# Low halves of the second layer's feed-forward weights by a sign-turned ScalarE cast and an accumulating transfer

## The chip, the cores and the metric

The kernel runs on one core of a Trainium2 chip. The metric is the device time of one execution in microseconds (us). The core has five engines that run on their own and meet through semaphores: TensorE (PE in the profile) for matrix products, with its weight loads shown apart as PEld; VectorE (DVE); ScalarE (ACT); GpSimd (POOL); and SyncE (SP), which here only issues transfers. Transfers between the chip's DRAM and the on-chip memory, and inside that memory, run on 16 DMA engines whichever engine issued them.

## The reference, cut to what matters

A decoder trunk of two layers on 512 tokens of width 1024, all in float32. Each layer is a token mixer, a layer norm, a feed-forward network and a second layer norm. The change touches the feed-forward network of the second layer alone:

```python
def sqrelu_mlp(x, w1, b1, w2, b2):
    return jnp.square(jax.nn.relu(x @ w1 + b1)) @ w2 + b2
...
ffn = sqrelu_mlp(x, ffn_w1[layer], ffn_b1[layer], ffn_w2[layer], ffn_b2[layer])
x = layer_norm(DEEPNORM_ALPHA * x + ffn, ln2_g[layer], ln2_b[layer])
```

`w1` is 1024 x 4096 and `w2` 4096 x 1024, so each layer has 32 MB of feed-forward weights.

## The kernel before, in words

**Split products.** TensorE multiplies in a rounded float32 format (fp32r). To keep float32 accuracy every operand is split in a high half, the value rounded to that format, and a low half, what the rounding lost. A product is the sum of three: high x high, high x low, low x high. So each weight, once loaded, goes through two instructions: ScalarE casts the raw tile to the high half (L101), VectorE subtracts the high half from the raw tile to get the low half (L102).

**Units, chunks and slots.** The class `Weights` hands out the weights in units of 128 x 1024 values (512 KB), in the order of use. `_prep` makes a unit ready: it fetches the raw chunk if it isn't there (L71, issued on SyncE), then the cast and the subtraction. A raw chunk lies in one of two buffers (`bufs=2` in `fetch`), so the load of a chunk waits until the chunk two before has been read by its last reader. The two halves lie in one of eight slots (three and five, `add_slots`), so a unit's cast waits until TensorE is done with the unit eight before. `next` asks for units up to `ahead`, here 5, in front of the one in use; the compiler that schedules the program may bring them forward on an engine's queue, up to the eight slots. Once compiled, each engine works its queue in that fixed order.

**The second layer's feed-forward.** It runs in five blocks of 8, 8, 6, 4 and 6 tiles of 128 hidden columns (`FFN_BLOCKS[1]`). In a block, the f tiles come first (`ffn1`, products at L225): a tile takes one unit of the first weight, 24 products, then ScalarE's Relu (L154), VectorE's square, ScalarE's cast (L215) and VectorE's low half (L216). The f tiles have two accumulation banks (`stp`), so the Relu of a tile must be over before the next tile but one begins. Then come the products with the second weight, named g (L1311), in the last block h (L1295), 8, 8, 6, 4 and 6 units of 24 products each, added by VectorE to the residual. The first six f tiles of block one use units that were split earlier and kept in DRAM; they are brought back by GpSimd transfers (L88). In the first block the residual is also turned by TensorE and copied back by ScalarE (L1287) before the g products.

The units of the first weight (key `"f11"`, 26 of them) have 128 columns of a chunk of 256, so two units share a 1 MB chunk and each partition's slice is eight pieces of 512 bytes. The units of the second weight (key `"f21"`, 32) are a chunk of 512 KB each, 4 KB in one piece on every partition.

**Order by hand.** Where a layer norm is near, `fence` keeps both instructions of a unit behind an instruction of the norm (`i0`, `i1`). It binds the scheduler only and adds no wait.

Of the kernel before, what the change touches and what calls it, by code (L numbers as in the profile page):

```python
# [9 lines left out]
F32 = mybir.dt.float32  # L10
# [3 lines left out]
ALU = mybir.AluOpType  # L14
# [29 lines left out]
KEEP_FROM = 8  # L44
AHEAD = (5, 4)
FJ = 3
BEFORE = (1, 3, 1, 2)
MIX_BUFS = (3, 4, 1, 3, 3)
WARM = 24
# [6 lines left out]
class Weights:  # L56
# [23 lines left out]
    def _prep(self, n):  # L80
        nc = self.nc
        while self.done < min(n, len(self.units)):
            key, src, nk, ncol, off, width = self.units[self.done]
            if key[0] == "split":
                pool, s = self.slots[self.done % len(self.slots)]
                w = tuple(pool.tile([P, nk, ncol], F32R, tag=f"w{x}{s}", name=f"w{x}{self.done}", bufs=1) for x in ("hi", "lo"))
                for x, d in zip(w, self.kept[key[1]]):
                    nc.gpsimd.dma_start(x, d)  # L88
                self.ready[self.done] = w
                self.done += 1  # L90
                continue
            self.fetch(self.done)
            raw = self.chunk[key][:, :, off : off + ncol]
            pool, s = self.slots[self.done % len(self.slots)]
            hi = pool.tile([P, nk, ncol], F32R, tag=f"whi{s}", name=f"whi{self.done}", bufs=1)
            lo = pool.tile([P, nk, ncol], F32R, tag=f"wlo{s}", name=f"wlo{self.done}", bufs=1)
            if key[0] == "q":
                i0 = nc.scalar.mul(hi, raw, 0.125).ins
                i1 = nc.vector.scalar_tensor_tensor(lo, raw, 0.125, hi.bitcast(F32), op0=ALU.mult, op1=ALU.subtract).ins
            else:  # L100
                i0 = nc.scalar.copy(hi, raw).ins  # L101
                i1 = nc.vector.tensor_sub(lo, raw, hi.bitcast(F32)).ins  # L102
            if self.fence:
                self.tc.add_manual_dep(i0, self.fence[0], NOSYNC, reason="behind the layer norm")
                self.tc.add_manual_dep(i1, self.fence[1], NOSYNC, reason="behind the layer norm")
            self.ready[self.done] = (hi, lo)
            self.done += 1
# [58 lines left out]
def kernel(ctx: ExitStack, tc: tile.TileContext, a: dict, out: bass.AP):  # L166
# [780 lines left out]
    def ln_to_x(ln, c0, c1, g, b, xs, others):  # L947

        r = ln.norm(X, c0, c1, others)
        for j in range(KT):  # L950
            y, (xh, xl) = X[j][:, c0:c1], (t_[:, c0:c1] for t_ in xs[j])
            stt(y, y, pv(g[0], g[1] + j), r, ALU.mult, ALU.mult)
            bj = pv(b[0], b[1] + j)
            la = act(xh, y, AF.Identity, bias=bj)
            lv = V.scalar_tensor_tensor(xl, y, bj, xh.bitcast(F32), op0=ALU.add, op1=ALU.subtract).ins
        W.fence = (la.name, lv.name)
# [62 lines left out]
    def tail_norm_lead(xk, name, bias, g, b, lead_n, lead_name, then=None):  # L1019
# [7 lines left out]
        lead = Lead(lead_n, xs, lead_name)  # L1027
        ln_to_x(ln, *HALVES[0], g, b, xs, [lambda n=n: t.run(n) for n in BEFORE[:2]])
        t.run(2 * KT - t.done)
        ln_to_x(ln, *HALVES[1], g, b, xs, [lambda n=n: lead.run(n) for n in BEFORE[2:]])  # L1030
        return xs, lead.finish()
# [170 lines left out]
    def normalised(h, j0, j1):  # L1202
# [12 lines left out]
        if j1 == KT:  # L1215
            out(KT - 1)
            if h == 0:
                W.fence = split_done[h, FJ]

# [161 lines left out]
```

## Time and profile before

| | |
|---|---|
| times shown | 1183.87 and 1185.64 us, median 1184.76 |
| span of the profiled execution | 1181.7 us, that is 2.2 to 3.9 under the times shown, which count what lies around the span; its own whole time is not listed apart from these |
| TensorE busy | 1154.5 us, 98% |
| VectorE, ScalarE, GpSimd busy | 752.0, 507.9, 66.5 us |
| second layer's feed-forward after its first six tiles | 851 to 1174 us of the span |
| transfers over the whole span | 169.60 MB |

The page gives the busy time of each engine, the span in slices, the transfer queues, the chain of work that ended last, and the costliest groups of instructions as "line engine operation out<-in". The trace behind it can be asked for one tile, for a stretch of time or for an engine's waits. A row with "<-" at its end tells what released the engine from its idle time. A duration of one instruction includes its pipeline, so two that follow one another can overlap by a tenth of a microsecond.

### The profile page before, as it was taken

What the parts mean: (1) busy time and instruction counts of PE and PEld (TensorE: products, weight loads), DVE (VectorE), ACT (ScalarE), POOL (GpSimd) and SP (SyncE); (2) the same over time, 40 slices, a digit from 0 to 9 for tenths busy, and PEclk for the clock granted to TensorE, in tenths of its full rate; (3) what the DMA queues carried; (4) which work ended last, traced back from release to release, by engine and by line L of the source; (5) the groups of instructions that cost most, each with busy time, mean ns of one, the idle gap of its engine ahead of it and who ended that gap; (6) DMA issues with size and microseconds to landing.
All of it is one profiled execution on the core that took longest, in us unless ns stands there. A gap on an engine that the chain in (4) does not pass through costs nothing.

```text
span 1181.7 us, 17927 instructions
## 1 busy us (share of the span) xinstructions
PE 1154.5 (98%) x7252; PEld 966.1 (82%) x7252; DVE 752.0 (64%) x1332; ACT 507.9 (43%) x802; POOL 66.5 (6%) x125
## 2 busy tenths in 40 slices
PE   9989999999999999999999999899999999999997
PEld 7777767799888888888999776699988888888885
DVE  7999875498546546546565999886933433434446
ACT  6857769345434435434323122662741422413220
POOL 1022210000000000000021110001000000000000
PEclk9999999999999999999999999999999999999999
DMA  8511221332689678788464641215242232323211
GB/s 211 166 55 50 81 81 46 109 114 72 223 292 299 228 281 298 249 292 290 134 213 153 205 164 58 68 44 172 90 143 72 89 125 72 109 91 104 78 47 72
DMA packets 132547, 169.60 MB, mean 144 GB/s; under 512 B 13874, under 2 KB 105778, under 8 KB 132464
## 3 DMA queue, kind: packets, MB, share of 16 engines
q1 hardware_dynamic: 123664, 136.96, 36.0%
q0 software_dynamic: 8640, 31.46, 7.9%
q8 instruction: 57, 0.93, 0.3%
q14 instruction: 26, 0.21, 0.1%
q10 hardware_dynamic: 160, 0.03, 0.0%
HBM read 132.12 MB, written 35.65 MB: 142 GB/s over the span
## 4 chain that ended last, share of the span: by engine, by line
PE 83%; ACT 2%; DVE 1%; DMA 1%; issue 1%; POOL 0%; SPq 0%; DVEq 0%; ACTq 0%
PE f L225 24%; PE g L1311 12%; PE acf L225 11%; PE fl L225 5%; PE tlb L225 4%; PE tld L225 4%; PE pv L225 3%; PE h L1295 3%; PE pg L225 3%; PE cw L1126 3%; PE tla L225 2%; PE pl L225 2%; PE acmo L225 1%; PE gg L225 1%; PE gv L225 1%
## 5 line engine op out<-in xcount | busy, mean ns | idle before, releaser
L102 DVE TENSOR_TENSOR wlo<-raw,whi 128x1024 fp32r<-128x1024 f32 x176 | 213.3, 1223 | 196.1 <-ACT whi L101 193.0
L101 ACT CAST whi<-raw 128x1024 fp32r<-128x1024 f32 x176 | 182.3, 1050 | 319.6 <-PE g L1311 107.0
L1311 PE MATMUL g<-whi,hh 128*128 128x512 f32 x208 | 81.7, 393 | 0.0
L1311 PE MATMUL g<-whi,hl 128*128 128x512 f32 x208 | 81.6, 392 | 0.0
L1311 PE MATMUL g<-wlo,hh 128*128 128x512 f32 x208 | 81.6, 392 | 0.0
L225 PE MATMUL f<-xah,whi 128*128 128x512 f32 x208 | 81.0, 390 | 0.0
L225 PE MATMUL f<-xdh,whi 128*128 128x512 f32 x208 | 81.0, 389 | 0.0
L225 PE MATMUL f<-xdl,whi 128*128 128x512 f32 x208 | 80.9, 389 | 0.0
L225 PE MATMUL f<-xal,whi 128*128 128x512 f32 x208 | 80.9, 389 | 0.0
L225 PE MATMUL f<-xdh,wlo 128*128 128x512 f32 x208 | 80.9, 389 | 0.0
L225 PE MATMUL f<-xah,wlo 128*128 128x512 f32 x208 | 80.9, 389 | 0.0
L225 PE MATMUL acf<-hh,whi 128*128 128x512 f32 x192 | 75.6, 394 | 0.0
L225 PE MATMUL acf<-hl,whi 128*128 128x512 f32 x192 | 75.5, 393 | 0.0
L225 PE MATMUL acf<-hh,wlo 128*128 128x512 f32 x192 | 75.4, 393 | 0.0
L215 ACT CAST hh<-fr 128x512 fp32r<-128x512 f32 x64 | 39.7, 621 | 59.1 <-DVE fr L353 59.1
L216 DVE TENSOR_TENSOR hl<-fr,hh 128x512 fp32r<-128x512 f32 x64 | 44.1, 690 | 31.1 <-ACT hh L215 31.1
L353 DVE TENSOR_TENSOR fr<-fr 128x512 f32<-128x512 f32 x64 | 43.6, 684 | 16.7 <-ACT fr L154 16.7
L357 DVE SCALAR_TENSOR_TENSOR cy<-hp,wdw,cy 128x512 f32<-128x512 f32 (+1 forms) x75 | 49.3, 657 | 0.8 <-ACT cy L154 0.8
L88 POOL DMA_DIRECT2D whi<-kepth x30 | 16.0, 535 | 549.5 <-PE tlb L225 385.9
L1311 PEld LDWEIGHTS g<-whi,hh 128*128 128x128 f32 x208 | 39.1, 188 | 8.8
L1311 PEld LDWEIGHTS g<-wlo,hh 128*128 128x128 f32 x208 | 39.1, 188 | 8.8
L1311 PEld LDWEIGHTS g<-whi,hl 128*128 128x128 f32 x208 | 39.0, 188 | 8.8
(631 smaller groups left out, 2891.9 us busy)
## 6 DMA issues: line engine op xcount, KB each, us to landing
raw<-in_ffn_w_dram SPq DMA_DIRECT2D x48, 1024.0 KB, 5.5
raw<-in_ffn_w_dram SPq DMA_DIRECT2D x32, 512.0 KB, 3.8
kepth<-whi SPq DMA_DIRECT2D x30, 512.0 KB, 3.2
keptl<-wlo SPq DMA_DIRECT2D x30, 512.0 KB, 9.2
whi<-kepth POOLq DMA_DIRECT2D x30, 512.0 KB, 3.6
wlo<-keptl POOLq DMA_DIRECT2D x30, 512.0 KB, 4.6
raw<-in_conv_w_pw_dram SPq DMA_DIRECT2D x12, 1024.0 KB, 6.5
raw<-in_mix_w_in_dram SPq DMA_DIRECT2D x16, 512.0 KB, 4.2
```

What stands on the lines that cost most here:

```text
L88: nc.gpsimd.dma_start(x, d)
L101: i0 = nc.scalar.copy(hi, raw).ins
L102: i1 = nc.vector.tensor_sub(lo, raw, hi.bitcast(F32)).ins
L215: i0 = S.copy(hi, src).ins
L216: i1 = V.tensor_sub(lo, src, hi.bitcast(F32)).ins
L225: ins = PE.matmul(ps[:, c0:c1], u[:, k, ksl], v[:, c0:c1], start=start and k == 0 and i == 0, stop=stop and k == n - 1 and i == 2).ins
L353: V.tensor_tensor(o, x, y, op=op)
L357: V.scalar_tensor_tensor(o, x, s, y, op0=op0, op1=op1)
L1126: PE.matmul(cps[j, c0][g][C, :], Ds[j][t // 16][R, t % 16, :], hps[j][R, t + c0 : t + c1], start=t < 4, stop=t >= n - 4, tile_position=(R. ...
L1295: PE.matmul(ps, u, v, start=k == 0 and i == 0, stop=k == nk - 1 and i == 2)
L1311: PE.matmul(pss[b], u, v[:, kk, :], start=k + kk == 0 and i == 0, stop=k + kk == nb - 1 and i == 2)
```

## The change

For the units of the two keys in `BY_DMA`, all of the second layer's feed-forward weights that are split there, the low half is made in another way. ScalarE writes minus the raw tile, rounded, into the low tile; then GpSimd issues a transfer from the raw tile onto the low tile that adds instead of overwriting. Minus the rounded value plus the value is what the subtraction gave. VectorE's subtraction falls away for these units. The instruction held by the fence (`i1`) is now the ScalarE one. The other weights are split as before.

```diff
+BY_DMA = ("f11", "f21")
...
                 i0 = nc.scalar.copy(hi, raw).ins
-                i1 = nc.vector.tensor_sub(lo, raw, hi.bitcast(F32)).ins
+                if key[0] in BY_DMA:
+                    i1 = nc.scalar.mul(lo, raw, -1.0).ins
+                    nc.gpsimd.dma_start(lo, raw, accum_op=ALU.add)
+                else:
+                    i1 = nc.vector.tensor_sub(lo, raw, hi.bitcast(F32)).ins
```

## The prediction

> **What bounds the kernel now.** I read the page's busy times, then busy time by stage, then the chain of waits that ended last.
>
> ```profile
> span 1181.7 us, 17927 instructions
> PE 1154.5 (98%) x7252; PEld 966.1 (82%) x7252; DVE 752.0 (64%) x1332; ACT 507.9 (43%) x802; POOL 66.5 (6%) x125
> ...
> 851.00:1140.00 289.00, 288.98 (x1282) 237.74 (x1281) 120.13 (x138) 91.42 (x115) 0.00 (x0) 1.00 0.31 98
> ...
> 865.90 44.28 PE g L1311 x192
> 910.18 43.52 PE f L225 x192
> ```
>
> TensorE is the chain. In the 289.00 us of the second layer's feed-forward it is busy for 288.98, while VectorE is busy for 120.13, ScalarE for 91.42 and GpSimd for nothing. The chain there is "f" and "g" products alone: a first-weight tile takes 43.52 / 8 = 5.44 us, a second-weight unit 44.28 / 8 = 5.54 us. VectorE's subtractions are off this chain, so their price can come back at most as the idle time of TensorE, 0.02 us here. The question is thus not what VectorE saves, but whether the new way delivers the low halves in time, and what it holds up.
>
> **What is removed and added.** The rows of the raw tiles in the second half of the trace, and the nearest rows for the new parts:
>
> ```profile
> L101 ACT CAST whi<-raw x58: 1035/1053/1061, 833.3 to 1129.2; 128x1024 fp32r<-128x1024 f32 x58
> L102 DVE TENSOR_TENSOR wlo<-raw,whi x58: 1214/1225/1228, 834.8 to 1130.3; 128x1024 fp32r<-128x1024 f32 x58
> ...
> L98 ACT ACTIVATE whi<-raw x4: 1045/1058/1063, 25.9 to 106.4; 128x1024 fp32r<-128x1024 f32 x4
> 809.45 0.54 POOL L88 DMA_DIRECT2D wlo<-keptl  x1
> ```
>
> The 58 units are the 26 of the first weight that are not kept and the 32 of the second. VectorE loses 58 x 1.225 = 71 us. ScalarE gains 58 scaled copies; the nearest row is the same shape times 0.125, 1.058 us, so 61 us, of which 58 x 0.96 (two such instructions start 0.96 apart, rows below) count: 91 + 56 = 147 of 289 us at most, still half idle. GpSimd gains 58 issues of 0.54 us or more. Nothing else stands in its queue: the last of its transfers (809.45) is over before the first new one. So what waits behind a waiting issue is only the next low half.
>
> The low half no longer needs the high one, only its own scaled copy. Per unit it is ready 0.96 + L after the high half where it was 1.23, with L the time from the issue of the accumulating transfer to its landing. TensorE takes a unit eight units later (eight slots), some 43 us, so L itself is hidden. What is not hidden is the **raw buffer**.
>
> ```profile
> SPq L71 <- DVE wlo L102: 743.9, 99, 257.8
> ...
> 942.68 1.05 ACT L101 CAST whi<-raw 128x1024 fp32r<-128x1024 f32 x1 [1.87 <-PE f L225]
> 943.64 0.68 ACT L154 ACTIVATE fr<-f,PV 128x512 f32<-128x512 f32 x1
> 945.62 0.62 ACT L215 CAST hh<-fr 128x512 fp32r<-128x512 f32 x1 [1.31 <-DVE fr L353]
> 948.12 1.05 ACT L101 CAST whi<-raw 128x1024 fp32r<-128x1024 f32 x1 [1.88 <-PE f L225]
> ...
> raw<-in_ffn_w_dram SPq DMA_DIRECT2D x8, 512.0 KB, 3.8
> ...
> raw<-in_ffn_w_dram SPq DMA_DIRECT2D x48, 1024.0 KB, 5.5
> ```
>
> SyncE's load of the next raw chunk waits for the last reader of the chunk two before, VectorE's subtraction today: that is the 743.9 us row. With the change the last reader is the accumulating transfer. And on ScalarE the cast of a unit stands ahead of the Relu of the tile just finished (942.68, then 943.64). A cast that waits for its load holds back the Relu, and TensorE has two banks for these tiles.
>
> While the f tiles run, the units cast are second-weight ones, a chunk of their own each. One buffer's round is then: cast and scaled copy 2 x 0.96 and a hand-over, 2.0; the transfer, L; the next load 3.8. It has to fit in two tiles, 10.88 us, so **L up to 5.1 us costs nothing**. Today the same round is 1.05 + 1.23 + 3.8 = 6.1.
>
> No accumulating transfer is in the trace. The rows around it, all 512 KB:
>
> ```profile
> q1 hardware_dynamic: 123664, 136.96, 36.0%
> q0 software_dynamic: 8640, 31.46, 7.9%
> ...
> kepth<-whi SPq DMA_DIRECT2D x30, 512.0 KB, 3.2
> keptl<-wlo SPq DMA_DIRECT2D x30, 512.0 KB, 9.2
> whi<-kepth POOLq DMA_DIRECT2D x30, 512.0 KB, 3.6
> wlo<-keptl POOLq DMA_DIRECT2D x30, 512.0 KB, 4.6
> ```
>
> Bounds for L are 3.2 us (out of SBUF, the first of a pair) and 9.2 us (out of SBUF, the second). I take 4.6: issued by GpSimd, onto the same tile, with another transfer in flight, which comes nearest. The round is then 2.0 + 4.6 + 3.8 = 10.4, inside 10.88: **0 us** in the steady stretches; at 9.2 it is 15.0, 4.1 too long.
>
> A page speaks against this. The Trainium skill, "Collectives: The Full Stack", section "The bandwidth ceiling: the fold count and why AG ≠ RS ≠ AR", says that an add in the DMA engine needs two source reads where a copy needs one, and that this halves the rate. By it the data part of the 3.6 us row (144 packets, 9 an engine, at 0.079 x 16 x 1181.7 / 8640 = 0.173 us, so 1.56 us) would count twice, L would be 5.2 and the round 11.0, late by 0.1 us: 12 rounds cost 1 us, inside ScalarE's slack. The sum stays as it is; no row here shows an add.
>
> **The start.** In the first block the prefetch is not yet ahead:
>
> ```profile
> 837.14 22.09 SPq L71 DMA_DIRECT2D raw<-in_ffn_w_dram  x7
> ...
> 833.30 1.98 ACT L101 CAST whi<-raw 128x1024 fp32r<-128x1024 f32 x2
> ...
> 840.81 1.05 ACT L101 CAST whi<-raw 128x1024 fp32r<-128x1024 f32 x1
> ...
> 862.59 1.05 ACT L101 CAST whi<-raw 128x1024 fp32r<-128x1024 f32 x1 [1.54 <-DMA raw<-in_ffn_w_dram]
> 863.54 0.68 ACT L154 ACTIVATE fr<-f,PV 128x512 f32<-128x512 f32 x1
> 864.12 1.55 ACT L1287 COPY X<-xt 128x512 f32<-128x512 f32 x3
> ...
> DMA raw<-in_ffn_w_dram: 4.5, 3
> ```
>
> The chunk of the first two units is free at 837.14 today. With the change its scaled copies end at 833.30 + 4 x 0.96 = 837.2, the second transfer is issued 0.54 behind the first and lands 4.6 later: 842.5. The load behind it lands at 846.3, and with rounds of 10.4 the units 3, 5 and 7 of the second weight are cast at 856.7, 867.1 and 877.5, where unit 7 is cast at 862.59 today. TensorE wants unit 7 at 865.90 + 7 x 5.54 = 904.7 and its low half is there by 884, so weights don't run out. But the Relu at 863.54 and the copies of the turned residual at 864.12, which the first g products need, stand on ScalarE behind these casts today. If that order stays, they wait until 879.5: **15 us**. If the late casts are ordered behind them: **0**. I take **4.5 us**, by the row of this very stretch that is nearest: three casts there wait 4.5 us in all for their loads, so the order lets a cast stand that much ahead of its data.
>
> **Sum.** Span 1181.7 + 0 (steady) + 4.5 (start) - 0.02 at best = 1186.2. The median shown, 1184.76, is 3.1 above the profiled span, so the forecast is **1189.3 us**.
>
> **The rivals.**
> Fully hidden: the order on ScalarE follows the loads and L is 5.1 or less. For it speaks that TensorE has 43 us of prefetch, against it the start. 1184.8 us.
>
> First-weight transfers are cut small. Their raw slice is 128 of 256 columns, eight pieces of 512 bytes a partition against one of 4 KB. If GpSimd's issue grows with the pieces it is 8 x 0.54 = 4.3 us; 64 pieces an engine at the 0.36 x 16 x 1181.7 / 123664 = 0.055 us of queue 1 are 3.5 us, 1.9 more than 1.56. L is then 4.6 + 3.8 + 1.9 = 10.3 for these. A chunk of two has 4 x 5.54 = 22.2 us and needs 5.5 (its load) + 5.54 (until the second unit's turn) + 2.0 + 10.3 = 23.3: 1.2 late, six rounds, 7 us. The start is 9.4 later, by the share taken above (4.5 of 15) 3 more, so 7. 1184.8 + 14 = 1199 us. Against it: 0.54 us for 128 pieces may be mostly fixed.
>
> Slower: the **round through the raw buffer becomes the bound** in the f tiles. At L = 9.2 it is 15.0 against 10.88. The f tiles of blocks 2 to 5 have 24 second-weight units cast in front of their Relus, 12 rounds x 4.1 = 49 us, less the slack: a Relu ends 2 x 0.96 + 0.68 = 2.6 after its tile and must be over by 5.44, so 2.8 in each of four blocks, 11. That leaves 38. The start has unit 7 cast at 850.9 + 3 x 15.0 = 895.9, a bound of 34, by the same share 10. 1184.8 + 48 = 1233 us. It begins at L = 5.1 and passes 2% (23.7 us, about what a measurement tells from no change) near 12 x (L - 5.1) - 11 + 6 = 23.7, so L = 7.5. For it: the 9.2 row, the transfer reads two tiles and writes one, and loads share the 16 engines (share 0.31 now). Against it: 9.2 is reached behind a sister transfer, and by a write to DRAM.
>
> Faster: only a rearranged order elsewhere could do it; TensorE idles 0.02 us in the stretch.
>
> The change does what it says by the code: minus the rounded weight plus the weight is the old low half.
>
> **How the numbers follow.** Forecast 1189.3: 0.40. Hidden, 1185: 0.14. Small pieces, 1199: 0.13. Buffer round, 1233: 0.32. Faster: 0.01. The first three lie within 2%: 0.67. The range runs from 1182.5 (hidden, and the spread of the two times) to 1238, just past the buffer's price; beyond it L above 9.2 is left out.
>
> **What would show it.** Right: 118 subtractions left at the old line; 58 scaled copies of 1.06 us; 58 issues on GpSimd and a landing near 4.6 us; SyncE's loads waiting for that transfer, not for VectorE; ScalarE's casts waiting for loads a few us more, all near 860; TensorE's idle time before the first g product only. Wrong: landings above 7 us, casts in every f stretch waiting for raw loads, and TensorE idle before f tiles with the Relu as releaser.

## The result and the profile after

The changed kernel takes **1244.29 us** (1244.08 to 1244.5), against 1184.76 before: a ratio of 1.0511, 95% interval 1.0471 to 1.0551. That is 59.5 us slower, past the upper end of the range. The page of the changed kernel, its busy times, the chain that ended last, and two of its transfer rows:

```profile
span 1242.8 us, 18061 instructions
PE 1166.1 (94%) x7252; PEld 971.4 (78%) x7252; DVE 684.9 (55%) x1274; ACT 559.2 (45%) x860; POOL 133.6 (11%) x183
...
PE 50%; DMA 25%; issue 7%; ACT 7%; DVE 7%; SPq 2%; POOL 1%; ACTq 0%; DVEq 0%; POOLq 0%
...
wlo<-raw POOLq DMA_DIRECT2D x58, 512.0 KB, 7.1
raw<-in_ffn_w_dram SPq DMA_DIRECT2D x32, 512.0 KB, 4.5
```

VectorE is relieved by 67 us (the sum had 71). But a quarter of the chain is now transfers, where before they were 1% of it and TensorE 83%. The adds land 7.1 us after their issue at the median, and the second-weight loads, 3.8 us in the same row before, take 4.5.

Busy time of the changed kernel in two stretches, the start of the second layer's feed-forward and what follows (columns as in the prediction: length, busy time of PE, PEld, DVE, ACT and POOL, granted clock, share of the DMA engines, GB/s):

```profile
851.00:910.00 59.00, 44.59 (x205) 37.05 (x204) 10.11 (x15) 32.55 (x43) 12.09 (x11) 0.88 0.75 162
910.00:1140.00 230.00, 197.07 (x824) 159.04 (x823) 37.30 (x54) 87.66 (x104) 41.60 (x35) 0.93 0.85 164
```

TensorE is idle for 14 us of the first and 33 us of the second. Before, it was idle for 0.02 us of both together. Who waits for whom in the changed kernel (total time in us, times, longest), and the casts of the 58 units, with what they waited for (total time in us, times):

```profile
PE f L230 <- ACT fr L159: 35.6, 9, 12.2
...
SPq L72 <- DMA wlo<-raw: 592.7, 43, 268.9
...
L102 ACT CAST whi<-raw x58: 1030/1047/1056, 830.7 to 1191.8; 128x1024 fp32r<-128x1024 f32 x58
...
  DMA raw<-in_ffn_w_dram: 186.2, 34
```

All 43 loads issued here wait for an adding transfer (the longest wait, 268.9 us, is that of the first load, which stood ready long before this stage). 34 of the 58 casts wait for a load, 186.2 us in all, where before it was 3 casts and 4.5 us. TensorE waits nine times for the Relu of an f tile. The casts stretch over 361 us; before it was 833.3 to 1129.2, 296 us, and there 48 of them waited for TensorE to free their slots. The two raw buffers are the bound now.

One round of a raw buffer, in the second block's f tiles. First the rows of ScalarE, then GpSimd's issue, then the load from the chain, then the landings of the adds from 946 to 995 us (smallest, median, largest):

```profile
970.66 1.05 ACT L102 CAST whi<-raw 128x1024 fp32r<-128x1024 f32 x1 [3.90 <-DMA raw<-in_ffn_w_dram]
971.61 0.68 ACT L159 ACTIVATE fr<-f,PV 128x512 f32<-128x512 f32 x1
972.19 1.05 ACT L104 ACTIVATE wlo<-raw 128x1024 fp32r<-128x1024 f32 x1
...
983.97 1.05 ACT L102 CAST whi<-raw 128x1024 fp32r<-128x1024 f32 x1 [3.25 <-DMA raw<-in_ffn_w_dram]
```

```profile
973.53 0.88 POOL L105 DMA_DIRECT2D wlo<-raw  x1 [6.15 <-ACT wlo L104]
```

```profile
980.00 3.88 DMA raw<-in_ffn_w_dram
```

```profile
DMA to landing us min/median/max: 4.5/6.3/7.6
```

The cast starts at 970.66. The scaled copy does not follow it: the Relu goes in between, and the add is issued at 973.53, 2.9 us after the cast. It lands 6.4 us later, the load starts at 980.00, and the next cast from this buffer is at 983.97. The round is 13.3 us, against 10.88 us for two tiles; the other rounds of this stretch are 11.9 to 14.1 us. And the Relu of each tile stands behind such a cast, as in the second row.

The first-weight units, two to a chunk, are worse. Casts at 1002.62 and again, from the same buffer, at 1027.61; GpSimd's issues in between, and their landings from 1004 to 1033 us:

```profile
1002.62 1.05 ACT L102 CAST whi<-raw 128x1024 fp32r<-128x1024 f32 x1 [8.48 <-DMA raw<-in_ffn_w_dram]
...
1027.61 1.06 ACT L102 CAST whi<-raw 128x1024 fp32r<-128x1024 f32 x1 [17.30 <-DMA raw<-in_ffn_w_dram]
```

```profile
1004.92 1.57 POOL L105 DMA_DIRECT2D wlo<-raw  x1 [10.00 <-ACT wlo L104]
...
1010.61 1.53 POOL L105 DMA_DIRECT2D wlo<-raw  x1 [0.35 <-ACT wlo L104]
```

```profile
DMA to landing us min/median/max: 7.1/9.4/15.7
```

That round is 25.0 us, where TensorE needs the four units of two chunks in 4 x 5.54 = 22.2. Taking 13.3 for each of the 32 second-weight chunks and 25.0 for each of the 13 first-weight ones, the two buffers need (32 x 13.3 + 13 x 25.0) / 2 = 375 us: near the 361 us over which the casts lie, and well over the 296 us that TensorE gives.

The start, where the turned residual is copied back:

```profile
876.54 1.97 PE L1289 MATMUL xt<-ident,X 128*128 128x128 f32 x8 [14.41 <-ACT X L1292]
```

```profile
874.44 1.04 ACT L102 CAST whi<-raw 128x1024 fp32r<-128x1024 f32 x1 [2.21 <-DMA raw<-in_ffn_w_dram]
875.39 0.61 ACT L220 CAST hh<-fr 128x512 fp32r<-128x512 f32 x1
875.91 4.05 ACT L1292 COPY X<-xt 128x512 f32<-128x512 f32 x8
```

TensorE waits 14.41 us for ScalarE's copies, which stand behind casts that wait for loads: the place that the prediction named, at its upper bound of 15 us.

### The profile page after: what moved, and what is told of

It reads as the page before. It is cut to its first block, busy times and chain, and to the rows that moved or that the text cites. A ratio compares the mean times of both kernels' runs of the same rounds, so it can differ in the third digit from the quotient of the medians.

```text
span 1242.8 us, 18061 instructions
## 1 busy us (share of the span) xinstructions
PE 1166.1 (94%) x7252; PEld 971.4 (78%) x7252; DVE 684.9 (55%) x1274; ACT 559.2 (45%) x860; POOL 133.6 (11%) x183
## 4 chain that ended last, share of the span: by engine, by line
PE 50%; DMA 25%; issue 7%; ACT 7%; DVE 7%; SPq 2%; POOL 1%; ACTq 0%; DVEq 0%; POOLq 0%
DMA raw<-in_ffn_w_dram 14%; PE acf L230 9%; PE f L230 9%; DMA wlo<-raw 9%; PE tlb L230 3%; PE tld L230 3%; PE pv L230 3%; ACT whi L102 2%; PE pg L230 2%; PE cw L1131 2%; PE h L1300 2%; DVE wlo L107 2%; PE tla L230 2%; PE pl L230 2%; PE acmo L230 1%
## 5 line engine op out<-in xcount | busy, mean ns | idle before, releaser
L107 DVE TENSOR_TENSOR wlo<-raw,whi 128x1024 fp32r<-128x1024 f32 x118 | 142.4, 1223 | 62.5 <-ACT whi L102 59.4
L230 PE MATMUL f<-xdh,whi 128*128 128x512 f32 x208 | 85.3, 410 | 35.6 <-ACT fr L159 35.6
L105 POOL DMA_DIRECT2D wlo<-raw x58 | 67.4, 1179 | 320.7 <-ACT wlo L104 291.9
L230 PE MATMUL f<-xdl,whi 128*128 128x512 f32 x208 | 83.8, 403 | 0.0
L230 PE MATMUL f<-xdh,wlo 128*128 128x512 f32 x208 | 83.6, 402 | 0.0
L358 DVE TENSOR_TENSOR X<-X,g 128x512 f32<-128x512 f32 x32 | 22.0, 688 | 110.1 <-PE g L1316 109.4
L230 PEld LDWEIGHTS f<-xdh,whi 128*128 128x128 f32 x208 | 40.9, 197 | 47.9 <-ACT fr L159 39.4
L104 ACT ACTIVATE wlo<-raw 128x1024 fp32r<-128x1024 f32 x58 | 61.0, 1052 | 0.0
```

The costliest lines, as they stand in the source:

```text
L104: i1 = nc.scalar.mul(lo, raw, -1.0).ins
L105: nc.gpsimd.dma_start(lo, raw, accum_op=ALU.add)
L230: ins = PE.matmul(ps[:, c0:c1], u[:, k, ksl], v[:, c0:c1], start=start and k == 0 and i == 0, stop=stop and k == n - 1 and i == 2).ins
L358: V.tensor_tensor(o, x, y, op=op)
```

## The experiments

Three theories stood. *Held buffer*: a raw buffer is held until the add has landed, so loads, casts, and the Relus behind them come late. *Full DMA engines*: the adds take more engine time than there is. *ScalarE*: its second pass over the raw tile delays the rest. Each run was timed beside the kernel before on the same chip; the ratio is to that, with its 95% interval. Runs quoted by number are counted in the order shown. The medians of before in the three groups of runs were 1183.34, 1183.82 and 1183.73 us.

**Only the second weight.**

```diff
-BY_DMA = ("f11", "f21")
+BY_DMA = ("f21",)
```

> Only the 32 second-weight units get the accumulating transfer (4 KB in one piece per partition, some 2.7 us of all 16 DMA engines each in the changed kernel); the 26 first-weight units are subtracted by VectorE as before. Theory 'held buffer' (the raw buffer is held until the transfer lands): rounds of 2.0 + 4.5 to 6.3 + 3.8 against 10.88 us, so at most 2 us late per pair of f tiles: 1185 to 1200 us. Theory 'full DMA engines' (the adds cost more engine time than there is): the full stretches are those of the first weight, so 1185 to 1190 us. Theory 'ScalarE' (the second pass over the raw tile delays the Relus): 32 of 58 passes stay, so 32/58 of the loss of 59.5 us, 1217 us.

Measured: 1196.8 us, ratio 1.0086 (1.0058 to 1.0114). Its software queue (packets, MB, share of the 16 engines) and the two stretches:

```profile
q0 software_dynamic: 13248, 48.24, 15.2%
...
851.00:910.00 59.00, 52.43 (x236) 43.38 (x236) 14.28 (x17) 25.79 (x33) 5.13 (x6) 0.94 0.67 179
910.00:1140.00 230.00, 226.84 (x986) 185.87 (x986) 68.38 (x87) 87.83 (x106) 18.95 (x22) 0.99 0.54 138
```

TensorE is idle for 6.6 us at the start, at a DMA share of 0.67, and for 3.2 us after it, at 0.54: full engines don't explain it. The number lies in the range of the held buffer, and 20 us under ScalarE's.

**Only the first weight.**

```diff
-BY_DMA = ("f11", "f21")
+BY_DMA = ("f11",)
```

> Only the 26 first-weight units get the accumulating transfer (eight pieces of 512 bytes per partition); the second-weight units are subtracted by VectorE as before. 'Held buffer': landings of 7 to 15 us hold a buffer of two units, the loads of the second-weight chunks behind it come late: 1210 to 1235 us. 'Full DMA engines': 8 units x 5 us of adds and 4 loads x 3.1 us are 52 us in a g stretch of 44 us, 8 us late in each of three long blocks, most of it made up in the f stretches, where now no adds run: 1190 to 1205 us. 'ScalarE': 26/58 of the loss, 1211 us.

Measured: 1191.85 us, ratio 1.006 (1.0036 to 1.0083).

```profile
q0 software_dynamic: 35680, 45.09, 17.9%
...
851.00:910.00 59.00, 52.37 (x237) 43.35 (x236) 16.31 (x21) 28.46 (x37) 8.65 (x6) 0.94 0.70 152
910.00:1140.00 230.00, 230.00 (x1009) 189.06 (x1007) 76.68 (x96) 87.18 (x104) 28.23 (x19) 1.00 0.69 137
```

The held buffer's number was a miss; full engines' fits. But after 910 us TensorE loses nothing, so the loss is at the start, where it is idle for 6.6 us. The miss is one of arithmetic: with 6.1 us rounds for the second weight the buffers need (32 x 6.1 + 13 x 25.0) / 2 = 260 us, under 296, so long first-weight rounds are made up. What had been left out is that the two weights share the buffers, so that their rounds have to be summed. The two halves lose 13.5 and 8.5 us, together the kernel loses 59.5: the costs don't add. That they pass a limit together is how I read it; ScalarE's 1211 us was a miss as well.

**Reading the weight again from DRAM.**

```diff
-                    nc.gpsimd.dma_start(lo, raw, accum_op=ALU.add)
+                    nc.gpsimd.dma_start(lo, src[:, :, off : off + ncol], accum_op=ALU.add)
```

> The accumulating transfer reads the weight from DRAM again instead of from the raw tile, so the raw tile is free after ScalarE's two reads; the 30 MB come twice from DRAM. 'Held buffer': the loads no longer wait for a landing, 1185 to 1200 us. 'Full DMA engines': the same adds and pieces, more DRAM reading, no gain or a loss, 1235 to 1260 us. 'ScalarE': unchanged, 1244 us.

Measured: 1190.87 us, ratio 1.0044 (1.0022 to 1.0067).

```profile
851.00:910.00 59.00, 54.25 (x270) 45.52 (x270) 10.35 (x16) 35.31 (x47) 15.97 (x12) 0.97 1.09 235
910.00:1140.00 230.00, 230.00 (x1008) 188.94 (x1008) 48.25 (x70) 107.07 (x126) 56.10 (x42) 1.00 0.98 188
```

The same 58 adds, more traffic, a DMA share of 0.98, and TensorE without a gap after 910 us. What was taken away is the hold on the raw buffer; the source of the adds changed with it. Held buffer; full engines fall. (The share is added up from the times of packets, and the 1.09 of the first row shows that it can pass 1: it does not simply say how full the engines are.)

**A third raw buffer.**

```diff
-    ... tag="raw", name=f"raw{i}", bufs=2)
+    ... tag="raw", name=f"raw{i}", bufs=2 if self.urgent else 3)
```

> A third raw buffer in the feed-forward stages, all else as changed. 'Held buffer': a round may take three tiles, 16.3 us, against 2.0 + 7 + 3.8: 1185 to 1200 us. 'Full DMA engines': only the waiting for a landing is saved, the engine time (26 x 5.0 + 13 x 3.1 + 32 x 4.3 us = 308 us in some 300 us) stays, 1200 to 1225 us. 'ScalarE': unchanged, 1244 us.

Measured: 1199.52 us, ratio 1.011 (1.0071 to 1.015).

```profile
851.00:910.00 59.00, 45.37 (x222) 38.06 (x222) 9.31 (x14) 31.74 (x42) 10.54 (x10) 0.88 0.90 203
910.00:1140.00 230.00, 230.00 (x1008) 188.94 (x1008) 45.64 (x66) 104.53 (x123) 50.29 (x42) 1.00 1.00 187
```

The time alone lies at the border of two theories; the stretches decide. After 910 us nothing is lost, at a DMA share of 1.00. The start keeps its 14 us, and why the third buffer doesn't help there was not taken apart.

**First-weight units as chunks of their own**, so that an add is one piece of 4 KB per partition.

```diff
-                units += units_of(f"f1{layer}", ..., 128), 256)
+                units += units_of(f"f1{layer}", ..., 128), 128 if layer else 256)
```

> All as changed, but a first-weight unit is loaded as a chunk of its own, 128 columns wide, so its accumulating transfer is one piece of 4 KB per partition instead of eight of 512 bytes (and its load from DRAM has pieces of 512 bytes). If the small pieces make the adds dear (5.0 against 2.7 us of all engines), the buffer rounds become 4.2 + 2.0 + 5 = 11.2 against 10.88 us in all stretches and the loss falls to that of the start and a little more: 1195 to 1210 us. If the pieces don't matter and holding two buffers through any landing does, about 1230 to 1244 us. 'ScalarE': unchanged, 1244 us.

Measured: 1239.21 us, ratio 1.0466 (1.0429 to 1.0503). Its software queue, its casts and the landings of its adds:

```profile
q0 software_dynamic: 16992, 61.87, 21.6%
...
L102 ACT CAST whi<-raw x58: 1030/1048/1121, 832.2 to 1186.4; 128x1024 fp32r<-128x1024 f32 x58
...
DMA to landing us min/median/max: 4.5/5.1/6.4
```

The landings are short now, 5.1 us at the median, and yet nearly the whole loss stays. Every unit is a chunk now, 58 rounds in place of 45, and the casts lie over 354 us: 58 / 2 = 29 rounds of 12.2 us, over the 10.88 to 11.08 that two units of TensorE's work take. So the loss does not need the small pieces. But this run also gave every first-weight unit a buffer to itself, and how much the pieces add to the 25.0 us round of the changed kernel it cannot tell.

**A plain copy in place of the add** (the low halves then hold the weight itself).

```diff
-                    nc.gpsimd.dma_start(lo, raw, accum_op=ALU.add)
+                    nc.gpsimd.dma_start(lo.bitcast(F32), raw)
```

> The transfer from the raw tile onto the low tile overwrites instead of adding, so the low halves hold the weight itself; everything else, the pieces and the holding of the buffer too, is as changed. If the second read of an add is what makes the landing late, L falls to some 3.6 us for the second weight and 5 for the first, the round is 9.4 of 10.88 us and only the start stays: 1190 to 1200 us. If the pieces and the fixed part of a landing are the cost, 1225 to 1244 us.

Measured: 1191.82 us, ratio 1.0068 (1.0049 to 1.0087).

```profile
q0 software_dynamic: 16992, 61.87, 15.1%
...
910.00:1140.00 230.00, 230.00 (x1008) 189.08 (x1007) 49.72 (x72) 108.13 (x128) 28.88 (x42) 1.00 0.57 190
```

The copies land 4.0 us after their issue at the median, and the round fits. For the price of a transfer, take the software queue: the kept weights have 8640 packets there and 0.079 x 1181.7 = 93.4 us of packet time before, spread over the 16 engines, and I count the rest to the new transfers. A copy then takes (0.151 x 1187.3 - 93.4) / 58 = 1.48 us, a second-weight add (0.152 x 1195.1 - 93.4) / 32 = 2.76 us, a first-weight add (0.179 x 1188.7 - 93.4) / 26 = 4.59 us.

The packets of the same rows show that this run took away two things. A first-weight add makes (35680 - 8640) / 26 = 1040 packets, but a copy makes (16992 - 8640) / 58 = 144, in both weights, as a second-weight add does. So the small pieces went with the add, other than the expectation says. Like with like are the copies here and the adds of the run before, 144 packets each: (0.216 x 1237.0 - 93.4) / 58 = 3.00 us against 1.48, a factor of 2.0. For the second weight, whose packets stay the same in number and size, the add's own price is thus the nearest explanation of the long round; for the first weight, add and pieces went together, and no run parts them in a chunk of two units.

The rule weighed in the prediction (the Trainium skill, "Collectives: The Full Stack", section "The bandwidth ceiling: the fold count and why AG ≠ RS ≠ AR") says that the add of a reduce step needs two source reads and so runs at half the rate of a copy. The page states it for rings of three and more ranks; here the factor of 2.0 agrees with it.

**ScalarE's second pass without the transfer** (the low halves stay minus the rounded weight).

```diff
-                    nc.gpsimd.dma_start(lo, raw, accum_op=ALU.add)
+                    pass
```

> ScalarE's second pass stays, the transfer is left out, so the low halves are minus the rounded weight and the raw buffer is free after ScalarE. 'Held buffer': nothing holds the loads, 1182 to 1186 us. 'ScalarE': the second passes in front of the Relus are the loss, above 1200 us.

Measured: 1183.78 us, ratio 0.9999 (0.9979 to 1.0019).

```profile
910.00:1140.00 230.00, 230.00 (x1010) 189.23 (x1009) 48.50 (x71) 108.49 (x131) 0.00 (x0) 1.00 0.30 94
```

Theory *ScalarE* falls: its 61 us of second passes cost nothing by themselves. The same run shows that VectorE's 71 us bring nothing.

**The first block subtracted by VectorE**, two raw buffers.

```diff
-                if key[0] in BY_DMA:
+                if key[0] in BY_DMA and not (key[2] < 1024 if key[0] == "f11" else key[1] < 8):
```

> The ten units of the first block (two of the first weight, eight of the second) are subtracted by VectorE as before; the 48 later ones are as changed, with two raw buffers. Of the loss of 59.5 us the start, where ScalarE's copies of the turned residual wait behind casts (TensorE idle 14 us from 851 to 910 in the changed kernel), goes and the later stretches keep theirs: 1220 to 1232 us. If the later losses only hand on the lateness of the start, it is 1184 to 1195 us.

Measured: 1203.42 us, ratio 1.0166 (1.0126 to 1.0206), between the two expectations. Its stretches, TensorE's waits for the Relus, and two casts in its second block's f tiles that follow each other in one buffer:

```profile
851.00:910.00 59.00, 59.00 (x276) 48.87 (x275) 15.59 (x20) 26.47 (x34) 10.80 (x7) 1.00 0.80 158
910.00:1140.00 230.00, 217.56 (x934) 176.63 (x932) 43.00 (x64) 96.66 (x117) 44.10 (x38) 0.98 0.90 178
...
PE f L230 <- ACT fr L159: 12.3, 5, 3.8
```

```profile
939.68 1.05 ACT L102 CAST whi<-raw 128x1024 fp32r<-128x1024 f32 x1
...
952.18 1.05 ACT L102 CAST whi<-raw 128x1024 fp32r<-128x1024 f32 x1
```

With a good start the rounds of this block are 12.5 us, still 1.6 over 10.88. The kernel loses 19.6 us. In the profiled run, whose span is 20.7 us longer than before, TensorE waits 12.3 us for Relus, five times, and its busy time grows by 7.0 us (1154.5 to 1161.5).

**Both remedies**: the condition of the last run and the three buffers of the fourth.

> Both remedies together: the ten units of the first block are subtracted by VectorE, and the 48 later ones have three raw buffers. If the whole loss is the raw buffers' time (a start that uses up the prefetch, then rounds longer than TensorE needs), both are gone: 1182 to 1187 us, not apart from before. If the adds cost something of their own that no buffer hides (their DMA engine time, ScalarE's second pass), 1190 us or more.

Measured: 1183.82 us, ratio 1.0001 (0.9983 to 1.0019).

```profile
866.00:910.00 44.00, 44.00 (x193) 35.93 (x192) 5.50 (x8) 16.50 (x19) 10.81 (x7) 1.00 0.87 134
910.00:1140.00 230.00, 230.00 (x1010) 189.21 (x1009) 48.39 (x71) 108.35 (x131) 46.65 (x41) 1.00 0.97 189
```

Forty-eight adding transfers, a DMA share of 0.97, and no loss at all. Nothing is gained either, though VectorE does 59 us less.

**The first block alone by transfer.**

```diff
-                if key[0] in BY_DMA:
+                if key[0] in BY_DMA and (key[2] < 1024 if key[0] == "f11" else key[1] < 8):
```

> The other half of the run that had the first block subtracted: only the ten units of the first block get the accumulating transfer, two raw buffers. The later rounds are those of before (6.1 us against 10.88), so a late start is made up there: only TensorE's idle time before the first g products stays, 1190 to 1198 us. With the 20 us of the other half that would be some 30 of the 59.5 us: the rest belongs to neither alone, it is the lead lost at the start that long rounds don't win back. If the first block alone is the cause, 1220 us or more.

Measured: 1197.23 us, ratio 1.012 (1.0103 to 1.0137).

```profile
866.00:910.00 44.00, 30.34 (x133) 24.99 (x132) 7.86 (x10) 19.99 (x26) 4.20 (x5) 0.81 0.73 186
910.00:1140.00 230.00, 230.00 (x1008) 188.99 (x1007) 97.38 (x112) 67.81 (x82) 0.00 (x0) 1.00 0.29 95
```

The start costs 13.5 us by itself, and where the later rounds are short nothing more is lost behind it. With the 19.6 us of the later blocks that is 33; the other 26 us come only with both. That rounds longer than TensorE's work start without a lead there is my reading; no trace adds up the 26 us.

## Why the prediction was wrong

**What held.** TensorE was the only bound, and VectorE's time was worth nothing: the run without the transfer shows it. That the raw buffer is what the change puts at risk, that SyncE's loads would wait for the adds, that the casts would hold back the Relus, and that the start would stall at the residual's copies, all stands in the rows above. It stood there as a rival at 0.32 with 1233 us. The mechanism is that one, but that its price was only 11 us short is luck: it came from L = 9.2, and at the 6.3 us that was measured in the f stretch the rival's own formula, 12 x (L - 5.1) - 11 + 6, gives 9 us, a kernel of 1194 us.

**The step that failed** is the value for L, "I take 4.6", and with it "0 us in the steady stretches". The bounds of 3.2 and 9.2 us held for the second weight (4.5 to 7.6 us in the stretch shown). Each term of the round was sized by an undisturbed row: hand-over 2.0, where the compiler put the Relu between cast and scaled copy and it took 2.9; L 4.6, where the median was 6.3 in the f stretch shown; load 3.8 (3.9 in the round shown). The sum of 10.4 was 0.5 us under the limit of 10.88, and the measured one is 13.3. A margin of 0.5 us in a sum of three borrowed prices is no margin; it deserved even odds at best. The 5.2 us that the prediction weighed, with the add's data counted twice, pointed the right way and was also under the 6.3 us of that stretch; what makes up the rest was not taken apart. In the forecast's sum, the 0 us of the steady stretches is 19.6 where they are measured alone, the 4.5 us of the start is 13.5, and for the 26 us that come only with both it had no term.

**The first-weight adds** were taken at 4.6 as well and their small pieces set aside as another rival. They land after 7.1 to 15.7 us in the stretch shown, several in flight. How much of that the pieces cost stays open: the fifth run has none and loses nearly as much, but with more rounds. GpSimd's issue was priced at up to 4.3 us; it is 1.53, against 0.88 for a whole piece.

**The start** was taken at 4.5 us between 0 and 15, by what casts waited for in the old order. Alone it costs 13.5 us. The order stayed such that the copies were behind casts whose loads were late, so the upper bound was the value.

**The rivals were priced one at a time.** The buffer's rival was charged only for the f stretches, with the slack of each block taken off anew. In the changed kernel the two buffers are short of time over the whole stage, with 375 us of rounds for 296, so the lag of the start, of the first weight and of the second can carry over from block to block. Rounds summed over a whole stage, against the time that TensorE gives it, show how near the limit was. At the forecast's L = 4.6 a second-weight round was 10.4 and a first-weight one 5.5 + 5.54 + 2.0 + 4.6 = 17.6 us: (32 x 10.4 + 13 x 17.6) / 2 = 281 us, just inside. With the 15.0 us of the buffer rival and the 23.3 us of the small pieces together it was 391 us, far outside.

The slower clock of TensorE is part of the price: see below.

## What to carry to other kernels

When work moves from a compute engine to a transfer, ask first what the transfer holds while it is in flight: here the source buffer, so the next load waited for the landing, not for the issue. Add up the rounds of each buffer over the whole stage and compare them with what the bounding engine gives; a single stretch can look safe where the stage is not. A third buffer, or a source that nobody waits for, took this cost away once the stage was running, though not all of it at the start; and as VectorE was off the critical path, nothing was won by relieving it.

## What the runs showed of the hardware

TensorE pays twice for a long gap. In the changed kernel, the first product after the idle time before 946.69 us:

```profile
946.69 0.79 PE L230 MATMUL f<-xdh,whi 128*128 128x512 f32 x1 [12.20 <-ACT fr L159]
```

It takes 0.79 us where this product takes 0.39 otherwise. The products behind it start 0.43 us apart until 951.97 us and 0.24 apart from there on; before the gap it was 0.23. And the granted clock of the stretch from 910 to 1140 us is 0.93 against 1.00. TensorE's busy time grows from 1154.5 to 1166.1 us for the same 7252 products: 11.6 of the 61.1 us that the span grew are slower products and not waiting. This agrees with the Trainium skill, "TensorE: Matmul & The Clock Gate", section "Part 1: The HAM clock gate (the "warmup" mystery)", which says that the clock is halved after an idle window and comes back after a busy one.

The 16 DMA engines can show a share of 0.97 to 1.00 for 230 us without TensorE losing any time (runs three, four and nine); such a share by itself says nothing of who waits.
